# A two-layer hybrid decoder on one core: sums of squares by TensorE, later sums for the second half, rotary swaps from ScalarE's queue, and other distances and rates

## The chip, the core and the metric

The kernel runs on one core of a Trainium2 chip. The core's engines are TensorE (PE, with its weight loads shown as PEld), VectorE (DVE), ScalarE (ACT), GpSimd (POOL) and SyncE (SP), which here only issues DMAs. Each engine runs its own instructions strictly in the order in which they stand in its queue and waits on semaphores for the others. The metric is the device time of one execution in microseconds.

## The reference

A trunk of two layers over 512 tokens of width 1024, followed by a final RMSNorm. Cut to what matters:

```python
for l in range(DEPTH):                       # 2
    sh1, sc1, g1, sh2, sc2, g2 = split(silu(c) @ ada_w[l] + ada_b[l], 6)
    h = rmsnorm(x, norm_mix_g[l]) * (1.0 + sc1) + sh1
    u = h @ w_in[l]                          # 1024 -> 2564
    fq, fk, fv, ff, pu, rq, rk, rv, rg, cu = split(u)
    y_fox  = forgetting attention, 4 heads x 64, log-sigmoid(ff) summed along time as a bias
    y_pool = causal means over 2, 4, 8, 16 tokens, minus the input, times a 64x64 matrix per group
    y_ret  = chunked retention, 4 heads x 64: rope(rq), rope(rk), decay, group norm, silu(rg)
    y_conv = silu(layernorm(causal depthwise conv, 31 taps, of a * sigmoid(gate)))
    x = x + g1 * (concat(y_fox, y_pool, y_ret, y_conv) @ w_out[l])
    h = rmsnorm(x, norm_ffn_g[l]) * (1.0 + sc2) + sh2
    x = x + g2 * ((silu(h @ ffn_w1[l]) * (h @ ffn_w3[l])) @ ffn_w2[l])
return rmsnorm(x, final_g)
```

All inputs and outputs are float32.

## The kernel before

The activations lie transposed: `xT` holds eight chunks of 128 channels (k = 0 to 7) by 512 tokens. Every large product is made of three matmuls in a fast 32-bit format (`mm3`): each operand is split into a rounded half (`yh`, `wh`, `ah`) and a remainder (`yl`, `wl`, `al`), and the products high by high, high by low and low by high are summed in a bank of PSUM. One tile of weights is fetched by SP into `raw` (two buffers), rounded by ScalarE into `wh` (L179) and subtracted by VectorE into `wl` (L184, "weight split"); four such tiles are held. A product of 512 tokens over 8 chunks is 24 matmuls (`one`); `group` does four products over the two halves of the tokens (0 to 255, 256 to 511), so that the second half can still be in the making while the first is used.

**Norms.** Three norms stand between the large products: one ahead of each feed-forward part and one between the layers (the last, final norm is made in another way). `Norm.chunk` is called when a chunk of `xT` is done. For each half of the tokens it squares the chunk on ScalarE and adds it to `acc` on VectorE (L524), eight chunks in a row. The sum over the 128 channels that are left is a matmul with a column of ones (`token_sums`, tile `aux`), then a power on GpSimd (`r`), then `spread` copies it to all partitions by matmuls with the identity. `finish` scales `xT` (L494, tile `qk`), adds the shift and rounds on ScalarE (L503, `yh`) and takes the remainders on VectorE (L507, `yl`). `sums` and `finish` are not run at once: they are put into `pending` with a count, and `flush(n)` takes n off the counts at fixed places between the matmuls. So a count sets where among TensorE's matmuls the sums and the spread stand. `finish` follows the sums by 24.

**Side work in the mixer part.** The four mixers are Python generators that run beside the projections. At each `slot()` a generator advances by its rate (`r_...` for layer 0, `q_...` for layer 1), whole steps at a time; `finish_bg` runs what is left of it on the spot. `conv_gen` issues the 31 taps for two tiles on VectorE (L819, tile `hc`), one tap a step, then mean, variance, scale and swish (L827 to L842). The output projection (`do_o`) starts with `finish_bg([cg])`. `fox_gen` computes the log of the forget gate (`log_forget`, tiles `ff`, last operation L859), makes four empty steps, sums it along time by matmuls (4x128), sends the result through DRAM (`cumd`) back as rows on all partitions (tiles `ah`, `al`), adds the causal mask (L885, `cumD`) and then runs scores (L900, L904), exponentials (L909), normalisation (L911), transposes and products with v. In layer 0 a further generator computes the gates of `ada_w` with TensorE, one column of `aux` a step (from tile `pw`), and adds the bias on VectorE (L357, `mod`) after eight.

**Rotary swaps.** `rope` needs a copy of its tile with the 32-row blocks exchanged in pairs. Four DMAs of 32 x 512 make it (`rx`, L965), issued by the engine that `KN["RD"]` names; then three VectorE operations follow (L966 to L968), and a fourth (L970) for the queries.

**Order.** From the end of layer 0's first projections on, TensorE's matmuls keep the order of the program; the other engines' queues are ordered by a scheduler that simulates the program when it is built.

Of the kernel before, what the change touches and what calls it, by code (L numbers as in the profile page):

```python
# [13 lines left out]
ALU = mybir.AluOpType  # L14
# [32 lines left out]
def trunk(ctx, tc, x, c, positions, ada_w, ada_b, norm_mix_g, norm_ffn_g, w_in, fox_fb,  # L47
# [52 lines left out]
    def f(ap):  # L100
        return ap.bitcast(F32)
# [400 lines left out]
    def mod_hi(l, i, k, u, v, y):  # L502
        A.activation(yh[k][:, u:v], y, AF.Identity, bias=shift(l, i, k), scale=1.0)  # L503

    def mod_lo(l, i, k, u, v, y):
        sh = shift(l, i, k)
        V.scalar_tensor_tensor(out=yl[k][:, u:v], in0=y, scalar=sh, in1=f(yh[k][:, u:v]), op0=ALU.add, op1=ALU.subtract)  # L507

    class Norm:
        def __init__(self, l, i):  # L510
# [2 lines left out]
        def chunk(self, k, a, b):  # L513
            for (u, v) in HALF:
                if u < a or v > b:
                    continue
                n = self.cnt.get(u, 0)
                if n == 0:
                    self.acc[u] = tmp("P", H2)
                    A.activation(self.acc[u], xT[:, k, u:v], AF.Square)  # L520
                else:
                    sq = tmp("PT", H2)
                    A.activation(sq, xT[:, k, u:v], AF.Square)
                    V.tensor_tensor(out=self.acc[u], in0=self.acc[u], in1=sq, op=ALU.add)  # L524
# [903 lines left out]
```

## Time and profile before

| what | value |
|---|---|
| median of 3 runs | 1266.83 us (1265.42 to 1266.85) |
| profiled execution | 1266.76 us, its span 1265.0 us |
| busy: PE, DVE, ACT, POOL | 1208.8, 733.4, 411.6, 75.0 us |
| mean granted clock of TensorE | 0.972 |
| mixer part of layer 0, of layer 1 | about 76 to 235 us, 693 to 830 us |
| norms | about 265 to 304, 640 to 682, 858 to 898 us |

A busy time is the union of the spans of an engine's instructions; where TensorE stands for over a few tenths of a microsecond, the row of the next instruction names the wait in brackets, and the engine and line that ended it. In rows of the timeline the columns are start, length (us), engine, line, operation, output<-inputs, form and count; "x4" merges four instructions, and a matmul of float32 operands is shown as two. In the table of windows each engine's busy time is followed by its count, and the last three figures are the granted clock, the DMA engines' busy share and GB/s. In lists of waits the figures are the total, the number of waits and the longest.

### The profile page before, as it was taken

What the parts mean: (1) busy time and instruction counts of PE and PEld (TensorE: products, weight loads), DVE (VectorE), ACT (ScalarE), POOL (GpSimd) and SP (SyncE); (2) the same over time, 40 slices, a digit from 0 to 9 for tenths busy, and PEclk for the clock granted to TensorE, in tenths of its full rate; (3) what the DMA queues carried; (4) which work ended last, traced back from release to release, by engine and by line L of the source; (5) the groups of instructions that cost most, each with busy time, mean ns of one, the idle gap of its engine ahead of it and who ended that gap; (6) DMA issues with size and microseconds to landing.
All of it is one profiled execution on the core that took longest, in us unless ns stands there. A gap on an engine that the chain in (4) does not pass through costs nothing.

```text
span 1265.0 us, 17346 instructions
## 1 busy us (share of the span) xinstructions
PE 1208.8 (96%) x6781; PEld 1008.6 (80%) x6781; DVE 733.4 (58%) x1295; ACT 411.6 (33%) x690; POOL 75.0 (6%) x146
## 2 busy tenths in 40 slices
PE   9998899897999999999998899997999999999997
PEld 8786677697888888888898777777988888888877
DVE  6777964466987355473465997657653333342333
ACT  5434344243332222122233344524332122222222
POOL 5411011001000000000000000100100000000000
PEclk8999899798999999999998999999999999999999
DMA  9766742124987345353232342122543333233321
GB/s 308 191 179 191 179 135 70 46 72 127 290 291 240 100 136 171 102 177 95 88 82 72 97 122 78 51 83 83 165 136 97 87 100 98 86 99 100 94 73 67
DMA packets 240873, 160.07 MB, mean 127 GB/s; under 512 B 7094, under 2 KB 221328, under 8 KB 240792
## 3 DMA queue, kind: packets, MB, share of 16 engines
q1 hardware_dynamic: 240616, 158.89, 42.6%
q8 instruction: 53, 0.87, 0.3%
q14 instruction: 28, 0.23, 0.1%
q10 hardware_dynamic: 176, 0.08, 0.0%
HBM read 154.74 MB, written 2.11 MB: 124 GB/s over the span
## 4 chain that ended last, share of the span: by engine, by line
PE 83%; DVE 7%; issue 1%; DMA 1%; ACT 1%; SPq 0%; POOL 0%; DVEq 0%; ACTq 0%
PE mm L59 74%; PE sm L59 7%; DVE wl L184 2%; DVE hc L819 1%; PE aux L59 1%; PE sm L64 1%; DVE yl L507 1%; DVE qk L494 1%; DMA al<-cumd 1%; DMA raw<-in_w_in 0%; DVE xT L1141 0%; ACT wh L179 0%; DVE P L524 0%; DVE hc L827 0%; DMA rx<-rx 0%
## 5 line engine op out<-in xcount | busy, mean ns | idle before, releaser
L179 ACT CAST wh<-raw 128x1024 fp32r<-128x1024 f32 (+3 forms) x196 | 198.7, 1014 | 612.1 <-PE mm L59 458.9
L59 PE MATMUL mm<-yh,wh 128*128 128x512 f32 (+1 forms) x984 | 376.0, 389 | 0.0
L59 PE MATMUL mm<-yh,wl 128*128 128x512 f32 (+1 forms) x984 | 371.1, 381 | 0.0
L59 PE MATMUL mm<-yl,wh 128*128 128x512 f32 (+1 forms) x984 | 350.2, 378 | 0.2 <-DVE yl L507 0.2
L184 DVE TENSOR_TENSOR wl<-raw,wh 128x1024 fp32r<-128x1024 f32 (+3 forms) x196 | 231.9, 1183 | 163.9 <-ACT wh L179 153.6
L59 PEld LDWEIGHTS mm<-yh,wh 128*128 128x128 f32 x984 | 189.4, 193 | 39.7 <-issue 6.1
L59 PEld LDWEIGHTS mm<-yh,wl 128*128 128x128 f32 x984 | 190.4, 194 | 36.6
L59 PEld LDWEIGHTS mm<-yl,wh 128*128 128x128 f32 x984 | 176.8, 189 | 34.6 <-issue 1.0
L59 PE MATMUL mm<-ah,wh 128*128 128x512 f32 (+1 forms) x508 | 188.0, 370 | 1.7 <-ACT ah L551 1.7
L59 PE MATMUL mm<-al,wh 128*128 128x512 f32 (+1 forms) x508 | 186.9, 368 | 0.0
L59 PE MATMUL mm<-ah,wl 128*128 128x512 f32 (+1 forms) x508 | 186.5, 367 | 0.0
L1141 DVE SCALAR_TENSOR_TENSOR xT<-mm,mod,xT 128x512 f32<-128x512 f32 (+1 forms) x84 | 56.6, 674 | 142.8 <-PE mm L59 142.8
L59 PEld LDWEIGHTS mm<-ah,wh 128*128 128x128 f32 x508 | 96.5, 190 | 19.2 <-ACT ah L551 2.4
L59 PEld LDWEIGHTS mm<-al,wh 128*128 128x128 f32 x508 | 96.5, 190 | 17.0 <-DVE al L552 0.4
L59 PEld LDWEIGHTS mm<-ah,wl 128*128 128x128 f32 x508 | 96.5, 190 | 16.8
L1331 DVE TENSOR_TENSOR t<-t,mm 128x512 f32<-128x512 f32 x42 | 28.8, 686 | 108.0 <-PE mm L59 107.9
L819 DVE SCALAR_TENSOR_TENSOR hc<-hp,cwT,hc 128x512 f32<-128x512 f32 x120 | 84.6, 745 | 0.1
L364 DVE SCALAR_TENSOR_TENSOR acs<-ada,cact,acs 128x512 f32<-128x512 f32 x98 | 73.4, 749 | 6.5 <-DMA ada<-in_ada_w 4.6
L473 POOL TENSOR_TENSOR r<-r,mhalf 128x2 f32<-128x2 f32 (+3 forms) x16 | 19.1, 1191 | 621.6 <-DVE r L481 603.3
L59 PE MATMUL mm<-wh,yh 128*128 128x256 f32 (+1 forms) x128 | 37.9, 296 | 0.0
L59 PE MATMUL mm<-wl,yh 128*128 128x256 f32 (+1 forms) x128 | 36.7, 287 | 0.0
L59 PE MATMUL mm<-wh,yl 128*128 128x256 f32 (+1 forms) x128 | 36.7, 287 | 0.0
(251 smaller groups left out, 1161.8 us busy)
## 6 DMA issues: line engine op xcount, KB each, us to landing
raw<-in_ffn_w SPq DMA_DIRECT2D x104, 512.0 KB, 3.9
ada<-in_ada_w SPq DMA_DIRECT2D x80, 512.0 KB, 5.4
raw<-in_w_in SPq DMA_DIRECT2D x32, 512.0 KB, 4.3
raw<-in_ffn_w SPq DMA_DIRECT2D x32, 448.0 KB, 3.5
ad<-in_ada_w SPq DMA_DIRECT2D x32, 256.0 KB, 5.5
raw<-in_w_out SPq DMA_DIRECT2D x32, 256.0 KB, 3.0
raw<-in_w_in SPq DMA_DIRECT2D x4, 520.0 KB, 4.6
xn<-in_x SPq DMA_DIRECT2D x4, 512.0 KB, 5.6
```

The source lines that it names most:

```text
L59: m = nc.tensor.matmul(*a, **kw)
L64: m = nc.tensor.transpose(*a, **kw)
L179: A.copy(h[:, 0:n], raw)
L184: V.tensor_tensor(out=lo[:, 0:n], in0=raw, in1=f(h[:, 0:n]), op=ALU.subtract)
L364: V.scalar_tensor_tensor(out=acc, in0=r, scalar=ck, in1=acc, op0=ALU.mult, op1=ALU.add)
L473: G.tensor_tensor(out=out_, in0=ms, in1=mhalf[:, 0:ms.shape[-1]], op=ALU.pow)
L494: V.scalar_tensor_tensor(out=y, in0=xT[:, k, u:v], scalar=gs[l][i][:, k:k + 1], in1=rs, op0=ALU.mult, op1=ALU.mult)
L507: V.scalar_tensor_tensor(out=yl[k][:, u:v], in0=y, scalar=sh, in1=f(yh[k][:, u:v]), op0=ALU.add, op1=ALU.subtract)
L819: V.scalar_tensor_tensor(out=hcs[j], in0=hps[j][:, t:t + S], scalar=cwT[:, l, j, t:t + 1], in1=hcs[j], op0=ALU.mult, op1=ALU.add)
L1141: V.scalar_tensor_tensor(out=xT[:, n, u:v], in0=b[:, u:v], scalar=mod[l][:, gcol + n:gcol + n + 1], in1=xT[:, n, u:v], op0=ALU.mult, op1=A ...
L1331: V.tensor_tensor(out=t_, in0=t_, in1=b3, op=ALU.mult)
```

## The change

`chunk` squares the last two chunks (k = 6 and 7 in order of arrival) into tiles of their own (`rP`) and adds them nowhere; `sums` then runs three matmuls for each 128 tokens, one for `acc` and one for each of the two tiles, instead of one. The count ahead of the sums is 56 for the second half of the tokens instead of 18. `rope`'s four DMAs are issued by ScalarE. `r_conv` is 1.6 instead of 1.3, and `fox_gen` makes 5 empty steps in layer 0 and 6 in layer 1 instead of 4. `mod_lo` has an engine argument that no call sets.

```diff
-KN = {... 'RD': 'sync', ... 'r_conv': 1.3, ...}
+KN = {... 'RD': 'scalar', ... 'r_conv': 1.6, ...}
...
-    def mod_lo(l, i, k, u, v, y):
+    def mod_lo(l, i, k, u, v, y, eng="V"):
...
                 if n == 0:
-                    self.acc[u] = tmp("P", H2)
-                    A.activation(self.acc[u], xT[:, k, u:v], AF.Square)
-                else:
+                    self.acc[u] = [tmp("P", H2)]
+                    A.activation(self.acc[u][0], xT[:, k, u:v], AF.Square)
+                elif n < KD - 2:
                     sq = tmp("PT", H2)
                     A.activation(sq, xT[:, k, u:v], AF.Square)
-                    V.tensor_tensor(out=self.acc[u], in0=self.acc[u], in1=sq, op=ALU.add)
+                    V.tensor_tensor(out=self.acc[u][0], in0=self.acc[u][0], in1=sq, op=ALU.add)
+                else:
+                    sq = tmp("rP", H2)
+                    A.activation(sq, xT[:, k, u:v], AF.Square)
+                    self.acc[u].append(sq)
                 self.cnt[u] = n + 1
                 if n + 1 == KD:
-                    pending.append([18, lambda u=u, v=v: self.sums(u, v)])
+                    pending.append([18 if u == 0 else 56, lambda u=u, v=v: self.sums(u, v)])
 
         def sums(self, u, v):
-            r = token_rsqrt(token_sums(self.acc[u], 2), 2, 1.0 / D, KN["TR"])
+            pt = aux_cols(2)
+            for t in range(2):
+                for q, src in enumerate(self.acc[u]):
+                    PE.matmul(pt[:, t:t + 1], src[:, t * P:(t + 1) * P], ones[:, 0:1], start=q == 0,
+                              stop=q == len(self.acc[u]) - 1)
+            r = token_rsqrt(pt, 2, 1.0 / D, KN["TR"])
             pending.append([24, lambda: self.finish(u, v, r)])
...
         lf = log_forget(l, v[:, :, 256:260])
-        for _ in range(4):
+        for _ in range(5 + l):
             yield
```

**TensorE, the norm ahead of layer 0's feed-forward part.** `yh_94` to `yh_101` are the eight chunks of `yh`; `mm_2902` to `sm_2905` are the four products of the group; `aux` takes the sums. Before, the second half's sums stand after chunk 3 of the first two products:

```order
L59 MATMUL mm_2903<-yh_97,wh_2787 128x256
L59 MATMUL mm_2903<-yh_97,wl_2789 128x256
L59 MATMUL aux<-ones,P_2634 128x1 x2
L59 MATMUL mm_2902<-yh_98,wh_2638 128x256
L59 MATMUL mm_2902<-yh_98,wl_2640 128x256
```

After, they stand behind chunk 4 of the other two:

```order
L59 MATMUL sm_2905<-yh_98,wh_2895 128x256
L59 MATMUL sm_2905<-yh_98,wl_2897 128x256
L59 MATMUL aux<-ones,P_2634 128x1
L59 MATMUL aux<-ones,rP_2879 128x1
L59 MATMUL aux<-ones,rP_2900 128x1
L59 MATMUL aux<-ones,P_2634 128x1
L59 MATMUL aux<-ones,rP_2879 128x1
L59 MATMUL aux<-ones,rP_2900 128x1
L59 MATMUL mm_2904<-yh_99,wh_2858 128x256
```

The sums moved from behind 16 matmuls of the group to behind 52, and there are six instead of two; the same holds in the other two norms.

**TensorE, the end of layer 0's mixer part.** `mm_2349` is the last projection, `hc` the conv tiles, `t_2416` its squares, `mm_2465` the first output product. Before:

```order
L59 MATMUL mm_2349<-yh_101,wl_1819 128x512
L59 MATMUL aux<-sel,pw_2383 128x1
L59 MATMUL sm_2411<-hc_1030,ones 128x512
L59 MATMUL sm_2411<-hc_1031,ones 128x512
L59 MATMUL sm_2422<-ident,r_429_2273 64x128 x8
L59 MATMUL aux<-ones,t_2416 128x1 x4
L59 MATMUL sm_2444<-ident,r_462_2441 128x128 x4
L59 MATMUL mm_2465<-ah_2345,wh_1986 128x512
```

After, the conv mixer's spread (`r_431_2278`) stands here, ahead of the last projection (`mm_2375`):

```order
L59 MATMUL aux<-sel,pw_2269 128x1
L59 MATMUL sm_2320<-ada_2194,cact 32x128 x8
L59 MATMUL sm_2331<-ident,r_431_2278 128x128 x4
L59 MATMUL sm_2354<-ident,r_376_2026 64x128 x8
L59 MATMUL sm_2368<-pl_2220,pw_2215 128x512
L59 MATMUL mm_2375<-yh_94,wh_1813 128x512
```

The mean, the sums and the spread moved out from between the last projection and the first output product: 60, 36 and 24 projection matmuls now lie between them and that product.

**VectorE, the first normalised scores of layer 0.** `hc` rows are conv taps, `rx` and `qk` rows rotary passes, ISA rows scores with their row minima; the last two rows of each piece are the normalisations of the first two heads. Before:

```order
L184 TENSOR_TENSOR wl_1213<-raw_1209,wh_1211 128x1024
L819 SCALAR_TENSOR_TENSOR hc_1030<-hp_792,cwT,hc_1030 128x512
L966 TENSOR_TENSOR qk_1217<-rx_1215,cos_t 128x512
L819 SCALAR_TENSOR_TENSOR hc_1031<-hp_797,cwT,hc_1031 128x512
L910 RECIPROCAL mx_1231<-mx_1231 128x1
L910 RECIPROCAL mx_1237<-mx_1237 128x1
L819 SCALAR_TENSOR_TENSOR hc_1030<-hp_792,cwT,hc_1030 128x512
L967 TENSOR_TENSOR rx_1218<-rx_1218,sin_t 128x512
L819 SCALAR_TENSOR_TENSOR hc_1031<-hp_797,cwT,hc_1031 128x512
L911 TENSOR_SCALAR P_1230<-P_1230,mx_1231 128x128
L911 TENSOR_SCALAR P_1236<-P_1236,mx_1237 128x128
```

After (its lines are ten further on: L910 and L914 are scores, L921 the normalisation):

```order
L829 SCALAR_TENSOR_TENSOR hc_1030<-hp_792,cwT,hc_1030 128x512
L829 SCALAR_TENSOR_TENSOR hc_1031<-hp_797,cwT,hc_1031 128x512
L910 ISA P_1344,mx_1345<-sm_1340,cumD_1226 128x128
L910 ISA mx_1345 128x1
L914 ISA P_1344,mx_1345<-sm_1340,ah_201_1168 128x128
L914 ISA mx_1345 128x1
L910 ISA P_1352,mx_1353<-sm_1341,cumD_1228 128x128
L910 ISA mx_1353 128x1
L914 ISA P_1352,mx_1353<-sm_1341,al_202_1169 128x128
L914 ISA mx_1353 128x1
L921 TENSOR_SCALAR P_1249<-P_1249,mx_1250 128x128
L921 TENSOR_SCALAR P_1255<-P_1255,mx_1256 128x128
```

The second pair's four score passes moved ahead of the first pair's normalisations; the ada bias add L357, which stood twelve rows behind them, now stands seven rows above this piece. In ScalarE's queue the swaps now stand as four DMAs each, right behind the copy that they read for the first, and behind exponentials and copies of the ada steps for the next three.

More of the change, by code (lines that the diff above doesn't have):

```diff
@@ L34 @@
 TW = 528
-KN = {'GA': 3, 'GA1': 3, 'TR': 'V', 'NH': 6, 'NH1': 6, 'ST': ((0, 1), (1, 1), (2, 2), (4, 1), (5, 1), (6, 1), (7, 1)), 'MO': 'rk rq rv pu rg o o o o', 'MO1': 'rk rq rv pu rg o o o o', 'GK': 4, 'RD': 'sync', 'MM': 3, 'SM': 4, 'FB': 1, 'FB1': 1, 'OUTP': 0.0, 'FRONT': 1, 'FRONT1': 0, 'r_rot': 2, 'r_ada': 0.9, 'r_conv': 1.3, 'r_fox': 1, 'r_ret': 1, 'r_pool': 1, 'r_adaV': 0.4, 'q_conv': 1.3, 'q_fox': 1, 'q_ret': 1, 'q_pool': 1, 'q_adaV': 1, 'bP': 4, 'bPT': 2, 'bt': 3, 'brx': 2, 'bmx': 6, 'br8': 4, 'bpl': 3, 'brP': 4, 'bada': 3, 'bacs': 2, 'NR': 2, 'NW': 4, 'N1': 2, 'N11': 1, 'YLG': 9, 'SC': ('AVPPPGPA', 'GGPAVVPP', 'VVVVVVPP', 'VVVVVGVP', 'AAVPAVVP', 'VVVVVVVP', 'VVVVVVVP', 'AAVPAVVP'), 'SH': ('AVAPPPPP', 'VPPPPPAP', 'AAGAAAPP', 'AAAAAAPP', 'AAAAAAGP', 'AVVGAAVG', 'AAAAAAPP', 'AAAAAAPP'), 'MS': '', 'OF': {'lc': -1.907, 'lwq': -2.817, 'lw': -2.364, 'lh': -2.036, 'sc': -1.65, 'ds': 0.034, 'sh': -2.846, 'pc': -0.763, 'mc': -2.466, 'ph': -0.991, 'mh': 0.907, 't': 0.871, 'yh': -1.858, 'yl': 0.927, 'wh': -0.208, 'wl': -2.386, 'whq': -1.469, 'wlq': -0.219, 'mm': 0.333, 'mq': -0.566, 'dq': 0.84}, 'KB': (-4.084, -0.552, 1.672, 3.163, 4.202, 4.915, 6.134, 7.492), 'OA': (1, 0, 2, 3), 'OA1': (0, 1, 3, 2), 'OB': (1, 2, 0, 3), 'OB1': (1, 3, 0, 2), 'OUTP1': 3.0}
@@ new lines @@
+KN = {'GA': 3, 'GA1': 3, 'TR': 'V', 'NH': 6, 'NH1': 6, 'ST': ((0, 1), (1, 1), (2, 2), (4, 1), (5, 1), (6, 1), (7, 1)), 'MO': 'rk rq rv pu rg o o o o', 'MO1': 'rk rq rv pu rg o o o o', 'GK': 4, 'RD': 'scalar', 'MM': 3, 'SM': 4, 'FB': 1, 'FB1': 1, 'OUTP': 0.0, 'FRONT': 1, 'FRONT1': 0, 'r_rot': 2, 'r_ada': 0.9, 'r_conv': 1.6, 'r_fox': 1, 'r_ret': 1, 'r_pool': 1, 'r_adaV': 0.4, 'q_conv': 1.3, 'q_fox': 1, 'q_ret': 1, 'q_pool': 1, 'q_adaV': 1, 'bP': 4, 'bPT': 2, 'bt': 3, 'brx': 2, 'bmx': 6, 'br8': 4, 'bpl': 3, 'brP': 4, 'bada': 3, 'bacs': 2, 'NR': 2, 'NW': 4, 'N1': 2, 'N11': 1, 'YLG': 9, 'SC': ('AVPPPGPA', 'GGPAVVPP', 'VVVVVVPP', 'VVVVVGVP', 'AAVPAVVP', 'VVVVVVVP', 'VVVVVVVP', 'AAVPAVVP'), 'SH': ('AVAPPPPP', 'VPPPPPAP', 'AAGAAAPP', 'AAAAAAPP', 'AAAAAAGP', 'AVVGAAVG', 'AAAAAAPP', 'AAAAAAPP'), 'MS': '', 'OF': {'lc': -1.907, 'lwq': -2.817, 'lw': -2.364, 'lh': -2.036, 'sc': -1.65, 'ds': 0.034, 'sh': -2.846, 'pc': -0.763, 'mc': -2.466, 'ph': -0.991, 'mh': 0.907, 't': 0.871, 'yh': -1.858, 'yl': 0.927, 'wh': -0.208, 'wl': -2.386, 'whq': -1.469, 'wlq': -0.219, 'mm': 0.333, 'mq': -0.566, 'dq': 0.84}, 'KB': (-4.084, -0.552, 1.672, 3.163, 4.202, 4.915, 6.134, 7.492), 'OA': (1, 0, 2, 3), 'OA1': (0, 1, 3, 2), 'OB': (1, 2, 0, 3), 'OB1': (1, 3, 0, 2), 'OUTP1': 3.0}
@@ L503, in mod_hi @@
         A.activation(yh[k][:, u:v], y, AF.Identity, bias=shift(l, i, k), scale=1.0)
-    def mod_lo(l, i, k, u, v, y):
+    def mod_lo(l, i, k, u, v, y, eng="V"):
         sh = shift(l, i, k)
-        V.scalar_tensor_tensor(out=yl[k][:, u:v], in0=y, scalar=sh, in1=f(yh[k][:, u:v]), op0=ALU.add, op1=ALU.subtract)
+        (G if eng == "G" else V).scalar_tensor_tensor(out=yl[k][:, u:v], in0=y, scalar=sh, in1=f(yh[k][:, u:v]),
+                                                      op0=ALU.add, op1=ALU.subtract)
     class Norm:
```

## The prediction

> **What bounds the kernel now.** I read the shares and the clock line of the page, then the waits of TensorE over the whole span, then a table by stage, then the rows inside four stages.
>
> ```profile
> PE 1208.8 (96%) x6781; PEld 1008.6 (80%) x6781; DVE 733.4 (58%) x1295; ACT 411.6 (33%) x690; POOL 75.0 (6%) x146
> PEclk8999899798999999999998999999999999999999
> PE 83%; DVE 7%; issue 1%; DMA 1%; ACT 1%; SPq 0%; POOL 0%; DVEq 0%; ACTq 0%
> ```
>
> TensorE is the bound: 96% busy, 83% of the chain that ended last. Time can come only from its waits and from its clock, which dips below full in some slices. This lists what it waits for:
>
> ```profile
> PE aux L59 <- DVE P L524: 18.3, 3, 6.5
> PE sm L59 <- DVE ff L859: 6.2, 2, 4.1
> PE aux L59 <- DVE t L832: 3.1, 1, 3.1
> PE aux L59 <- DMA rx<-rx: 2.9, 1, 2.9
> PE mm L59 <- ACT ah L551: 1.7, 1, 1.7
> ```
>
> Three waits for the norm's adds (L524), two for the forget gate's logarithm (L859), the tail of the conv mixer (L832, L551), one named after a rotary swap: 32.2 us, and all of them stand where the diff works. The stages around them:
>
> ```profile
> core 0: us, PE busy (x) PEld busy (x) DVE busy (x) ACT busy (x) POOL busy (x), PEclk, DMA share, GB/s
> 127.00:140.00 13.00, 10.39 (x63) 7.38 (x64) 11.78 (x33) 3.33 (x9) 0.37 (x2) 0.74 0.61 150
> 140.00:155.00 15.00, 14.55 (x141) 11.51 (x140) 15.00 (x41) 6.51 (x17) 0.84 (x3) 1.00 0.74 193
> 200.00:219.60 19.60, 18.68 (x161) 14.56 (x160) 6.81 (x13) 6.09 (x13) 1.90 (x3) 1.00 0.23 70
> 219.60:235.40 15.80, 9.74 (x46) 7.03 (x45) 8.80 (x16) 6.66 (x11) 1.21 (x2) 0.66 0.12 36
> 235.40:265.00 29.60, 29.60 (x114) 23.52 (x115) 12.63 (x15) 4.73 (x6) 0.00 (x0) 0.89 0.23 71
> 720.00:735.00 15.00, 14.90 (x69) 11.40 (x70) 15.00 (x24) 2.15 (x4) 0.00 (x0) 0.90 0.32 102
> ```
>
> The third figure from the end is the granted clock: 0.74 behind the 2.9 us wait, which ends at 129.6, 0.66 and 0.89 around the conv tail, 0.90 after the layer-1 logarithm. So a wait costs its length and then some matmuls at a lower clock. VectorE is full in 140 to 155 and in 720 to 735, and a third busy just ahead of the conv tail.
>
> **The norms: squares and the later sums.** Rows of the first norm (after layer 0's output projection):
>
> ```profile
> 275.27 0.55 PE L59 MATMUL aux<-ones,P 128*128 128x1 f32 x4
> 275.68 0.37 PE L59 MATMUL mm<-ah,wh 128*128 128x256 f32 x1
> 284.59 0.28 PE L59 MATMUL mm<-yh,wh 128*128 128x256 f32 x1
> 284.71 0.28 PE L59 MATMUL mm<-yh,wl 128*128 128x256 f32 x1
> 291.46 1.01 PE L59 MATMUL aux<-ones,P 128*128 128x1 f32 x4 [6.48 <-DVE P L524]
> 292.70 0.41 PE L59 MATMUL mm<-yh,wl 128*128 128x256 f32 x1
> 292.91 0.41 PE L59 MATMUL mm<-yh,wh 128*128 128x256 f32 x1
> 304.15 0.28 PE L59 MATMUL mm<-yh,wh 128*128 128x256 f32 x1
> 288.01 1.22 DVE L184 TENSOR_TENSOR wl<-raw,wh 128x1024 fp32r<-128x1024 f32 x1
> 289.93 1.48 DVE L524 TENSOR_TENSOR P<-P,PT 128x256 f32<-128x256 f32 x3
> 297.77 3.22 DVE L494 SCALAR_TENSOR_TENSOR qk<-xT,gs,sm 128x256 f32<-128x256 f32 x8 [5.09 <-PE sm L59]
> 300.91 3.25 DVE L507 SCALAR_TENSOR_TENSOR yl<-qk,mod,yh 128x256 fp32r<-128x256 f32 x8
> ```
>
> TensorE does 16 matmuls of the first half, then stands 6.5 us at the second half's sums, whose last three adds sit on VectorE behind a weight split (288.01) and the first half's remainders. Matmuls start 0.12 us apart before (284.59 to 284.71) and 0.21 after (292.70 to 292.91). The matmuls of the second half start at 304.15, and its first 24 end at 304.15 + 24 x 0.118 = 307.0.
>
> Moved: the sums stand behind 52 matmuls instead of 16, the spread behind 24 more as before. Two of the three adds at 289.93 go (0.4 us each). Added: six sum matmuls for two; two took 0.41 us (275.27 to 275.68), so four more are 0.8 us a half. I follow the new order with these durations. The 16 matmuls that end at 284.8 began at 284.83 - 16 x 0.118 = 282.9; now 0.8 us late, at 283.7. Its matmuls of the fourth tile begin 35 places on, at 287.9, but that tile's split ends about 289.4: 1.5 us of new wait, which the old stall hid. Then 16 matmuls to the sums, at 291.4. The one add left follows the split and two remainders, 289.4 + 0.9 + 0.4 = 290.7, so no wait. Sums 1.2, 24 matmuls 2.8, spread 0.4: 295.8; 20 matmuls: 298.2. Scaling (8 x 0.40) runs from 296.0, the rounded halves follow at that pace, the last at 299.8, just when wanted. The remainders run 299.2 to 302.5 and are wanted from 300.1 to 300.9: another 1.6 us. The first 24 matmuls end near 302.6 against 307.0: 4.4 us. The other two norms have the same code and waits that make 18.3 with this one; taken as 4.3 each, three norms give 13 us. Ends: 7.4 each if neither new wait appears (6.5, plus 22 matmuls x 0.095, plus 0.4 on the slow sums, less 1.6), 2 each if both double: 6 to 22.
>
> The clock: after 6.5 us of standing, 22 matmuls ran at half rate. The Trainium skill ("TensorE: Matmul & The Clock Gate", Part 1) says an idle window of about 3.4 us halves the clock, and about 3.4 us of work restores it; the 0.21 us agree, but the 2.9 us wait was followed by 0.74 as well. By that rule alone a 2.9 us wait would cost no clock, the 13 x 0.26 below would not come back, and the sum would be some 3 us smaller; the row decides, and I keep it.
>
> **Conv tail, layer 0 (r_conv 1.3 to 1.6).**
>
> ```profile
> 219.80 1.96 PE L59 MATMUL sm<-hc,ones 128*128 128x512 f32 x4
> 221.70 1.09 PE L59 MATMUL sm<-ident,r 128*64 128x128 f32 x16
> 229.05 2.07 PE L59 MATMUL sm<-ident,r 128*128 128x128 f32 x8 [1.34 <-POOL r L473]
> 230.78 0.77 PE L59 MATMUL mm<-ah,wh 128*128 128x512 f32 x1
> 241.79 0.43 PE L59 MATMUL mm<-ah,wl 128*128 128x512 f32 x1
> 235.33 1.30 DVE L552 TENSOR_TENSOR al<-hc,ah 128x512 fp32r<-128x512 f32 x2
> ```
>
> Today the generator has steps left when the projection wants its result, so mean, variance, scale and swish are forced out in a row with TensorE waiting. Between 219.80 and 241.79 it does the mean (1.9), a spread for retention (1.1), four sums (4 x 0.2 = 0.8), the conv spread (1.7 at half clock, so 0.9), and 20 matmuls of 512 columns (twice 0.118: 4.7): 9.4 us of work in 22.0. Now mean, sums and spread stand 60, 36 and 24 projection matmuls ahead. The 24 take 5.6 us, with some 2 us of small ones among them; spread to the last remainder takes 229.05 to 236.6, 7.6 us, and VectorE there was a third busy (6.81 of 19.60). So nearly all 12.6 us come back; I take 11.5, leaving 1 us for VectorE finishing pool, retention and conv together. Ends: 8 and 12.6.
>
> **Forget gate (5 + l steps).**
>
> ```profile
> 103.48 0.38 PE L59 MATMUL sm<-cs,ff 128*4 128x128 f32 x2 [2.13 <-DVE ff L859]
> 720.10 0.59 PE L59 MATMUL sm<-cs,ff 128*4 128x128 f32 x2 [4.10 <-DVE ff L859]
> 730.57 0.69 DVE L885 TENSOR_TENSOR cumD<-al,cs 128x512 f32<-128x512 f32 x1
> 739.40 0.29 DVE L900 CUSTOM_DVE_ANT_0 P<-sm,cumD 128x128 f32<-128x128 f32 x1
> PEld aux L59 <- DVE mod L357: 3.1, 1, 3.1
> L965 SPq DMA_DIRECT2D rx<-rx x32: 507/584/1576, 114.7 to 766.0; - x32
> SPq L965 <- DVE qk L968: 7.5, 3, 3.3
> ```
>
> Layer 1: 24 more matmuls (5.6 us) stand ahead of the cumulative sum, over the 4.1 us. Its scores keep their place, so the path from the sum through DRAM to the scores loses 5.6 us of cover; its last decay add ended at 731.3 and the scores read it at 739.4, so that holds. Gain 4.1 + 15 x 0.10 of clock = 5.6; VectorE is full behind it but its queue holds fewer taps ahead of the scores, so 5. Ends 1 and 5.6.
>
> Layer 0: one step more (12 projection matmuls and an ada step, 3.7 us) covers the 2.1. Here the scores move with it. Between decay and the first normalised scores VectorE's queue now holds four more score passes (0.3 each, as at 739.40), two rotary passes and a tap (0.65 each, as in the pair at 235.33): 3.2 us, so I put a wait of 2 us at the transposes. In return the 2.9 us wait goes: the page names the swap as its end, but the weight load of the same matmul names the ada bias add L357, which stood behind scores and a weight split and now stands ahead of them. Before: 2.1 + 2.9 + 13 x 0.26 of clock = 8.4; after: 2 + 2 of clock. Gain 4, ends -4 (the wait at the transposes as long as the norm's) and 8.4.
>
> **Swaps on ScalarE.** 32 issues of 0.58 us, four to a swap: 18.7 us move from SP to ScalarE, with SP's waits for L968 (7.5 us) in front of three of them. SP is relieved: weight and ada loads no longer queue there, worth nothing on the path since no wait of TensorE names a weight load here. On ScalarE, weight casts, score exponentials and PSUM copies queue behind each swap's 2.3 us. ScalarE is busy 6.51 of 15.00 in the densest stage. I take 2 us lost; ends 0 and 19. The Trainium skill ("DMA: Bandwidth & Descriptors", Issuing engines are not separate DMA queues) says another issuing engine saves only issue time; by that alone the swaps gain nothing, which is what the sum has.
>
> The other edits change no instruction (the engine argument is unused).
>
> **Sum.** 13 + 11.5 + 5 + 4 - 2 = 31.5 us off the profiled execution's 1266.76 (span 1265.0), which is 0.07 us under the median of 1266.83: 1235 us.
>
> **Rivals.** (1) VectorE becomes the bound in the mixers: full in 140 to 155 and 720 to 735, it keeps TensorE where it was, and the 9 us of the gate terms go: 1244. Against: its queue is no longer ahead of the weight splits in layer 1. (2) The second half of the norm comes too late: spread at 295.8 leaves 2.4 us before its matmuls; if scaling starts 4.4 us late (splits or casts in between), each norm gives nothing: 1248. (3) Slower: ScalarE is held by the swaps. If each stops it for 2.3 us and three also for L968, and all of it reaches TensorE, 18.7 + 7.5 = 26 us are lost where I took 2: 1259, and eight clock drops of 2.1 us (22 x 0.095, as after the norm's wait) make it 1276. It decides once a swap delays a PSUM copy by more than the 3 to 4 us that stand between a copy and its reader. (4) The waits have other releasers than named (the adds merely came last) and move on unchanged: 1266.
>
> **Chances.** Forecast 1235 (1225 to 1242) 0.65; rival 1 0.17; rival 2 0.10; rival 3 0.04; rival 4 0.04. The range holds forecast and rival 1 and rival 2: 1225 to 1250. Within 0.2% (2.5 us) is about what a measurement here can't tell from no change. Faster 0.93, same 0.03, slower 0.04.
>
> **What would show it.** After: the three L524 waits gone, with 1 to 2 us waits of TensorE for a split (L184) and the remainders (L507) in their place; no wait for L832 and a clock near 1.0 where 0.66 stood; no wait for L859; a wait of about 2 us at a transpose in layer 0 near 127; swaps on ScalarE's queue. A wait of TensorE for ScalarE copies of over 1 us at each swap, or a clock under 0.9 inside the norms, would make it wrong.

## The result, and the profile after

The changed kernel takes 1255.95 us (median of 4 runs, 1253.05 to 1256.45) against 1266.12 us for the kernel before (4 runs): a ratio of 0.9918 [0.9897, 0.9939]. By the ratio it is 10.4 us faster, where 31.5 were forecast. Two executions far slower than all others (one of the version q_nc below at 3004 us, which is also the one that its trace shows, so that trace is not used, and one of the kernel before at 4869 us) are left out of the ratios. The profiled execution took 1255.64 us, its span is 1253.9 us, its mean granted clock 0.981 (0.972 before).

The shares and the clock line of the page of after, and the longest waits of TensorE over its span (total, number, longest):

```profile
PE 1211.4 (97%) x6829; PEld 1009.3 (80%) x6829; DVE 726.6 (58%) x1283; ACT 410.7 (33%) x690; POOL 75.2 (6%) x146
PEclk7999898999999999999999999999999999999999
```

```profile
PE sm L59 <- DVE wl L184: 6.3, 3, 2.3
PE sm L64 <- DVE P L921: 5.3, 4, 2.9
PE aux L59 <- ACT pw L430: 4.5, 2, 2.4
PE sm L59 <- DVE qk L980: 2.9, 1, 2.9
PE sm L59 <- DVE mx L914: 1.4, 1, 1.4
```

All five waits that the prediction listed (32.2 us) are gone. In their place stand these five kinds, 20.4 us, of which the first was forecast. (Line numbers behind L526 are ten higher than before: L911 is now L921, L859 is L869.) TensorE is still the bound.

Cut at the same instructions in both traces, the stages changed by these lengths (from the rows' start times):

| stage | change, us |
|---|---|
| mixer part of layer 0, with output projection | -5.4 |
| first norm | -3.1 |
| second norm (between the layers) | -1.2 |
| mixer part of layer 1, with output projection | +1.0 |
| third norm | -1.9 |
| both feed-forward parts | 0.0 |

So the first layer's mixer part and the three norms improved, and layer 1's mixer part got worse. Of the 5.4 us of layer 0, some 1.5 are not the change's: before runs at half clock from 74.5 to 78 us, ahead of all that was edited, and after does not there, while p_conv and n56 below do. First the **norm ahead of layer 0's feed-forward part**, rows of the timeline of after:

```profile
283.09 1.22 DVE L184 TENSOR_TENSOR wl<-raw,wh 128x1024 fp32r<-128x1024 f32 x1
284.36 0.39 PE L59 MATMUL sm<-yh,wl 128*128 128x256 f32 x1 [2.02 <-DVE wl L184]
286.48 0.28 PE L59 MATMUL aux<-ones,P 128*128 128x1 f32 x2
287.74 0.36 PE L59 MATMUL mm<-yh,wh 128*128 128x256 f32 x1
293.48 0.28 PE L59 MATMUL mm<-yh,wh 128*128 128x256 f32 x1
295.54 2.61 PE L59 MATMUL mm<-yl,wh 128*128 128x256 f32 x8
297.98 0.28 PE L59 MATMUL mm<-yh,wh 128*128 128x256 f32 x1
```

The sums no longer wait, and take 1.26 us (286.48 to 287.74). The fourth tile's split comes 2.02 us late, and eight matmuls with remainders take 2.44 us (295.54 to 297.98) for some 0.94 of work: the two new waits that the prediction named. It had put them at 1.5 and 1.6 us; they are 2.0 and 1.5.

**The mixer part of layer 0**, a table by stage and the rows of TensorE's new waits:

```profile
127.00:142.00 15.00, 11.73 (x82) 8.32 (x81) 12.73 (x40) 4.99 (x13) 0.90 (x2) 0.95 0.77 202
142.00:156.00 14.00, 13.91 (x118) 11.82 (x119) 13.20 (x32) 4.42 (x13) 1.05 (x2) 0.81 0.48 133
200.00:215.00 15.00, 13.61 (x105) 11.15 (x106) 6.18 (x24) 4.02 (x10) 3.86 (x7) 0.79 0.24 73
230.00:275.00 45.00, 45.00 (x275) 39.52 (x274) 25.89 (x43) 12.13 (x22) 0.90 (x2) 1.00 0.23 72
```

```profile
117.79 0.38 PE L59 MATMUL aux<-sel,pw 128*128 128x1 f32 x2 [2.35 <-ACT pw L430]
124.46 0.38 PE L59 MATMUL aux<-sel,pw 128*128 128x1 f32 x2 [2.11 <-ACT pw L430]
140.89 0.87 PE L64 MATMUL sm<-ident,P 128*128 128x128 f32 x3 [2.88 <-DVE P L921]
182.41 0.64 PE L59 MATMUL sm<-ada,cact 128*32 128x128 f32 x16 [1.39 <-DVE mx L914]
201.02 0.64 PE L59 MATMUL sm<-ada,cact 128*32 128x128 f32 x16 [1.53 <-issue]
```

The conv tail is clean (230 to 275: TensorE busy throughout at clock 1.00, where 0.66 and 0.89 stood). The first half of the mixer is not: two waits for a copy on ScalarE (L430), one of 2.88 us for the normalised scores (L921), and two further on. The prediction had put a wait of 2 us at a transpose near 127, for passes that stand ahead of the normalisation. The one at 140.89 is another: VectorE itself stands for the second swap shortly ahead of it.

```profile
133.37 0.69 DVE L977 TENSOR_TENSOR rx<-rx,sin_t 128x512 f32<-128x512 f32 x1 [2.27 <-DMA rx<-rx]
```

The copies came late for this reason (ScalarE's rows; ACTq is its queue issuing DMAs):

```profile
109.78 7.65 ACTq L975 DMA_DIRECT2D rx<-rx  x4
116.92 0.51 ACTq L975 DMA_DIRECT2D rx<-rx  x1
117.47 0.27 ACT L430 COPY pw<-sm 128x128 f32<-128x128 f32 x1 [7.73 <-DMA ah<-cumd]
```

The first swap's four DMAs last from 109.78 to 117.43; at the 0.58 us of an issue on SP before, they would take 2.3. The fourth starts at 116.92, when the broadcast of the forget gate's sums from DRAM (`ah<-cumd`, issued by SP) has landed, and the copy behind it is put down to that transfer too. ScalarE's queue stands still for the 5.3 us of difference.

**Layer 1**: the wait for the logarithm (4.10) is gone; two others appeared, for the scores and for a rotary:

```profile
741.41 0.77 PE L64 MATMUL sm<-ident,P 128*128 128x128 f32 x4 [1.48 <-DVE P L921]
757.77 0.49 PE L59 MATMUL sm<-qk,qk 64*128 64x128 f32 x4 [2.88 <-DVE qk L980]
```

### The profile page after: what moved, and what is told of

Same layout as the page of the kernel before. It is cut to its first block, busy times and chain, and to the rows that moved or that the text cites. A ratio compares the mean times of both kernels' runs of the same rounds, so it can differ in the third digit from the quotient of the medians.

```text
span 1253.9 us, 17394 instructions
## 1 busy us (share of the span) xinstructions
PE 1211.4 (97%) x6829; PEld 1009.3 (80%) x6829; DVE 726.6 (58%) x1283; ACT 410.7 (33%) x690; POOL 75.2 (6%) x146
## 3 DMA queue, kind: packets, MB, share of 16 engines
HBM read 154.74 MB, written 2.11 MB: 125 GB/s over the span
## 5 line engine op out<-in xcount | busy, mean ns | idle before, releaser
L59 PE MATMUL mm<-yh,wl 128*128 128x512 f32 (+1 forms) x984 | 366.9, 378 | 0.0
L59 PE MATMUL mm<-yl,wh 128*128 128x512 f32 (+1 forms) x984 | 355.5, 380 | 0.2
L59 PEld LDWEIGHTS mm<-yh,wl 128*128 128x128 f32 x984 | 187.5, 191 | 36.7
```

The costliest lines, as they stand in the source:

```text
L59: m = nc.tensor.matmul(*a, **kw)
```

## The experiments

Diffs are against the kernel before unless another is named. A ratio is to runs of the kernel before on the same chip, with its 95% interval; one ratio can be told from another to some 0.003, or 4 us. In microseconds a ratio is taken times 1265.

**Each part alone.** p_norm has the diff's `chunk` and `sums`, with

```diff
-                    pending.append([18, lambda u=u, v=v: self.sums(u, v)])
+                    pending.append([18 if u == 0 else 56, lambda u=u, v=v: self.sums(u, v)])
```

> The kernel before with the norms' part alone (squares of the last two chunks by TensorE, the second half's sums at 56). In the trace of the whole change the three norms give 3.1, 1.2 and 1.9 us from the first half's sums to the second half's second product, 6.2 us together where I had predicted 13. Theory N1 (the split of the fourth tile comes late in VectorE's queue whatever else is changed): a wait of TensorE of 2.0 to 2.3 us for L184 in each norm, and 5 to 8 us off the kernel before: 1258 to 1261. Theory N2 (the splits are late only because the rest of the change shifts VectorE's queue): the L184 waits are under 1 us, the gain is 11 to 14 us, about 1253.

Measured: 1261.34 us, 0.9969 [0.9954, 0.9985]: 3.9 us, a little less than theory N1 gave. The waits are N1's; the split is late whatever stands around the norms:

```profile
PE sm L59 <- DVE wl L184: 6.3, 3, 2.3
```

is p_norm's row of waits, as in after.

```diff
-KN = {... 'r_conv': 1.3, ...}
+KN = {... 'r_conv': 1.6, ...}
```

> The kernel before with r_conv 1.6 alone. Theory C1 (the tail comes back as predicted): 8 to 12.6 us gained, 1254 to 1258, no wait at the sums of the conv squares, no low clock between 220 and 245. Theory C2 (the taps issued sooner take VectorE's time from the scores and weight splits before it): the tail's 9 us are gained and 3 to 8 us of it lost between 110 and 200, so 1258 to 1264.

Measured: 1255.62 us, 0.9928 [0.9907, 0.9948]: 9.1 us (theory C1), nearly as much as the whole change's 10.4.

```diff
-        for _ in range(4):
+        for _ in range(5 + l):
```

> The kernel before with the longer distance ahead of the cumulative sum alone (5 empty steps in layer 0, 6 in layer 1). My prediction: 9 us gained, 1257. Theory S (the swaps on ScalarE take away what the gates give): here, with the swaps on SP, 6 to 9 us are gained, and no wait of over 1.5 us stands at the transposes of the scores. Theory V (the scores come closer to other VectorE work and wait there): both waits for the logarithm go, but waits of 1.5 to 3 us for the normalised scores (L911) come in both layers; the gain is 0 to 3 us, 1263 to 1267.

Measured: 1271.52 us, 1.0059 [1.0038, 1.0080]: slower by 7.5 us, which neither theory gave. The steps cost where they should have gained. In this trace most of it stands in layer 1: from the first sums of the norm ahead of it to those of the norm behind it 221.9 us pass, 216.3 in before. TensorE's waits there grew by 1.1 us only; low clock took 9.6 us of its busy time instead of 4.8 (the last section says how this is counted).

```diff
-KN = {... 'RD': 'sync', ...}
+KN = {... 'RD': 'scalar', ...}
```

> The kernel before with the swaps issued by ScalarE alone. In the trace of the whole change the fourth DMA of the first swap starts 5.3 us late, when the broadcast of the cumulative sums has landed, and the copy of the ada sums behind it is waited for by TensorE for 2.4 us. Theory S: 5 to 10 us lost, 1271 to 1276, with waits of TensorE for L430. Theory V (the swaps cost ScalarE time that nobody waits for): within 2.5 us of the kernel before.

Measured: 1276.49 us, 1.0090 [1.0073, 1.0107]: slower by 11.4 us, theory S's time. Its sign did not come: no wait of TensorE for L430 stands among those of over 0.4 us, and no swap of layer 0 holds ScalarE longer than 3.01 us (the first 2.52). The new waits are for scores on VectorE (1.76 us at 140.81, 2.05 at 143.27) and for copies of transposed scores.

**In pairs.** q_nc is norms and conv, q_fs the steps and the swaps.

> The norms' part and r_conv 1.6 together, swaps on SP and 4 empty steps as before. Alone they measured 3.9 us (0.31%) and 9.1 us (0.72%) off. Theory I1 (these two are independent, and the other two parts, which cost 7.5 and 11.4 us alone, cancel each other inside the whole change): they add, 13 us off, 1251 to 1254. Theory I2 (norms and conv gain only together with the rest): 5 us off or less, 1260.

Measured: 1249.32 us (median of all four executions), 0.9874 [0.9850, 0.9898]: 15.9 us faster, some 3 more than the two parts alone add up to (theory I1, within the error), and better than the whole change by 5.6.

> The longer distance and the swaps on ScalarE together, norms and conv as before. Alone they cost 7.5 us (0.59%) and 11.4 us (0.90%). Theory I1: together they cost 0 to 5 us, 1265 to 1270. Theory I2: they add, 19 us, 1284.

Measured: 1274.16 us, 1.0064 [1.0041, 1.0088]: 8.1 us slower, between the two theories. The two pairs add up to -7.8, the whole is -10.4: additive within the error. So the change is two halves of opposite sign.

**Which of the two costs more.** a_sync is after with `'RD': 'sync'`; a_fox4 is after with `range(4)`; f0 and f1 are q_nc with one step more in layer 0 and two in layer 1:

```diff
-        for _ in range(4):
+        for _ in range(5 - l):        # f0
+        for _ in range(4 + 2 * l):    # f1
```

> The whole change with the swaps back on SP. Theory S (ScalarE held by the swaps ate what was missing, the fourth DMA waiting 5.3 us for the broadcast's landing): 8 to 12 us faster than the whole change, 1244 to 1248. Theory I1 (without the swaps' shift the longer distance costs its 7.5 us): 3 to 6 us slower than the whole change, 1259 to 1262.

Measured: 1254.84 us, 0.9926 [0.9900, 0.9951]: neither theory's time.

> The whole change with 4 empty steps in both layers, swaps on ScalarE. Theory S: the waits for the logarithm come back (2.1 and 4.1 us), 6 to 9 us slower than the whole change, 1262 to 1265. Theory I1: the swaps alone cost their 11.4 us against norms and conv alone: 1262 to 1265 too, with waits of 1 to 2 us for normalised scores at 125 and 140. Theory V (the distance costs by bringing the scores closer to other VectorE work, and the swaps cost little): 2 to 6 us faster than the whole change.

Measured: 1257.37 us, 0.9948 [0.9929, 0.9966]: 4 us slower than the whole change, which again no theory gave.

> Norms and conv together (1249) with 5 empty steps in layer 0 and 4 in layer 1. My prediction had layer 0's step gain 4 us: 1245. Theory V (the scores come closer to other work on VectorE and ScalarE): the waits of 2.1 and 2.9 us go, waits of 2.3 us for L430 and 1 to 1.5 us for scores come in their place, 1249 to 1252.

Measured: 1255.41 us, 0.9930 [0.9907, 0.9954]: slower still than theory V had it.

> Norms and conv together (1249) with 4 empty steps in layer 0 and 6 in layer 1. My prediction had layer 1's steps gain 5 us: 1244. Theory V: the wait of 4.1 us for the logarithm goes, waits of 1.9 us for the normalised scores near 743 and of 2.9 us for a rotary pass near 766 come, each followed by low clock: 1251 to 1255.

Measured: 1252.73 us, 0.9903 [0.9873, 0.9934]: theory V.

On top of q_nc (0.9874) the swaps alone cost 9 us, the step in layer 0 7, the steps in layer 1 4 (no more than the error), all steps 7, and everything 6. The costs don't add: with the steps in, putting the swaps back on SP changes nothing (0.9926 against 0.9918). The trace of f0 shows why, in rows of TensorE, ScalarE and SP:

```profile
127.76 0.59 PE L59 MATMUL aux<-sel,pw 128*128 128x1 f32 x2 [3.19 <-ACT pw L430]
125.16 0.59 ACT L1221 COPY rx<-mm 128x512 f32<-128x512 f32 x1 [4.97 <-DMA rx<-rx]
125.77 1.28 ACT L919 ACT_TABLE_LOAD   x1
127.46 0.25 ACT L430 COPY pw<-sm 128x128 f32<-128x128 f32 x1
115.20 0.57 SPq L889 DMA_DIRECT2D ah<-cumd  x1
117.30 2.51 SPq L975 DMA_DIRECT2D rx<-rx  x4
```

With the sum a step later its broadcast stands on SP's queue (115.20) just ahead of a swap (117.30). ScalarE's copy of the next tile into `rx` waits 4.97 us for a swap, the table load and an exponential follow, and the copy that TensorE wants (L430) stands behind them. So swap and broadcast meet on SP as they do through ScalarE's queue in after, and end in the same 2 to 3 us wait. (That the swap lands late because of the broadcast ahead of it is read from the order of the rows, and was not tested alone.) The wait is the smaller part of the loss: layer 0's mixer part is 7.9 us longer in f0's trace than in f1's, which leaves it alone, 2.5 of them TensorE's waits and 4.8 low clock. The rows of f1 in layer 1, where the logarithm's wait had been taken away:

```profile
725.87 0.33 PE L64 MATMUL sm<-ident,P 128*128 128x128 f32 x1 [2.34 <-DVE P L921]
750.34 1.64 PE L59 MATMUL sm<-qk,qk 64*128 64x128 f32 x16 [2.49 <-DVE qk L980]
```

That is 4.8 us of new waits for 4.1 (the logarithm's wait of 2.1 in layer 0 stays), and layer 1's part is as long as f0's, where its steps are not changed: 215.9 us in both.

**The sum later, the scores kept in place** (on n56, below): the step that stood behind the broadcast's DMAs is taken out in layer 0.

```diff
-        for _ in range(4):
+        for _ in range(5 - l):
...
-        yield
+        if l:
+            yield
```

> The version with conv and the later sums alone (1246.2), layer 0's cumulative sum one step later, but one empty step fewer behind it, so that the scores keep their place. Theory P (the scores' place costs: the last of them run out of projections to hide behind): the wait of 2.1 us for the logarithm goes and no waits come between 150 and 215: 1242 to 1246. Theory Q (the sum's way through DRAM loses its cover): the scores wait for the broadcast, 3 us or more at the first transposes: 1248 to 1252.

Measured: 1249.16 us, 0.9879 [0.9855, 0.9903], against n56's 0.9857: no gain, theory Q's time. No wait over 1 us stands between 150 and 215 us now, where f0 has three (1.13 at 157.63, then 1.39 and 1.54), but two stand ahead:

```profile
119.83 1.08 PE L59 MATMUL sm<-ada,cact 128*32 128x128 f32 x16 [4.40 <-issue]
129.15 0.59 PE L64 MATMUL sm<-ident,P 128*128 128x128 f32 x2 [4.19 <-DVE P L912]
```

Theory Q's cause is not shown, though. VectorE waits 5.88 us for the broadcast, as in before (5.93), and ScalarE's copy waits 5.86 us for the swap that now follows the broadcast directly, with the exponentials behind it. Which of the two holds the scores stays open; a step taken out behind the broadcast has at any rate not paid for the one put in ahead of it.

**Why the swaps cost on ScalarE.** When the issuing engine changes, the scheduler also orders VectorE and ScalarE in another way. pin_d and pin_da are q_nc with the swaps on ScalarE and a written-out order that holds VectorE (pin_d), or VectorE and ScalarE (pin_da), to that of q_nc:

```diff
-KN = {... 'RD': 'sync', ...}
+KN = {... 'RD': 'scalar', ...}
...
+        for order in PIN.values():
+            for p, q in zip(order, order[1:]):
+                tc.add_manual_dep(ins[q], p, NOSYNC, reason="pin")
```

> Norms and conv with the swaps on ScalarE (1257.4), but all instructions of VectorE and ScalarE beside the swaps themselves in the order that they have with the swaps on SP (1249.3). Only the 32 issues are moved. Theory S (the held queue costs): 1254 to 1259, with waits of TensorE for ScalarE's copies (L430, L932). Theory V (the changed order costs): 1248 to 1251, without the waits of 1.7 to 2.1 us at 128 and at 142 to 146.

Measured: 1254.75 us, 0.9929 [0.9907, 0.9951]: theory S's time.

> The same with VectorE's order alone forced back, ScalarE's left to the build. Theory S: 1254 to 1259. Theory V, if VectorE's order is the whole of it: 1248 to 1251; if ScalarE's counts too: between, 1251 to 1255.

Measured: 1254.31 us, 0.9924 [0.9909, 0.9940]: theory S's time too, or the one between.

Of the 9 us that the swaps cost on q_nc (0.9948), some 6 to 7 remain with the order held and 2 to 3 come back; the second figure is within the error. Rows of pin_da (lines two higher than in after; the traced execution took 1260.61 us, above the median):

```profile
114.55 4.00 ACTq L977 DMA_DIRECT2D rx<-rx  x4
709.73 0.59 PE L61 MATMUL sm<-cs,ff 128*4 128x128 f32 x2 [5.16 <-DVE ff L871]
750.81 0.93 PE L61 MATMUL sm<-PT,v 128*64 128x128 f32 x8 [2.11 <-ACT PT L934]
```

The first swap holds ScalarE 4.0 us, and in layer 1 the logarithm's wait is 5.16 instead of 4.10 and a copy of transposed scores (PT) is 2.11 late. From the totals one would say that the held queue carries most of the loss. But what remains is not the same loss. The table has one trace each: layer 0's mixer part from TensorE's wait at 73 us to the first norm's first sums, and the stretch with layer 1's, from the second norm's first sums to the third's; in brackets what low clock took of it. Swaps on SP are read from f1 for layer 0 and from f0 for layer 1, each of which leaves that part as in q_nc.

| us | layer 0 | layer 1 |
|---|---|---|
| swaps on SP | 189.2 (6.6) | 215.9 (2.0) |
| on ScalarE, order of the scheduler (a_fox4) | 196.8 (8.0) | 216.1 (1.7) |
| on ScalarE, VectorE's order held (pin_d) | 190.2 (6.6) | 219.0 (4.3) |
| on ScalarE, both orders held (pin_da) | 193.0 (8.3) | 221.2 (3.1) |

With the scheduler's own order the loss, 7.6 us, stands in layer 0, and layer 1 shows next to none. With VectorE's order held 6.6 of the 7.6 are gone, and so are the waits of 1.7 to 2.1 us at 130 and at 143 to 146 that theory V named, though the swaps still stand on ScalarE. No swap of layer 0 is held there (2.53 us for the first, where after has 7.65). So layer 0's loss goes with VectorE's changed order. Forced into the other order, layer 1 loses 3 to 5 us that it did not lose before; the rows of pin_da show a late ScalarE there, but how much of this is the held queue, the held order or the clock stays open.

n_pool issues them from GpSimd instead (on n56, below): `'RD': 'gpsimd'`.

> The version with conv and the later sums alone (1246.2), swaps issued by GpSimd, which is busy for 6% only. Theory S (ScalarE held by the issues): no loss, 1245 to 1248. Theory V (another issuer alters VectorE's order at the scores, whichever it is): 4 us lost or more, 1250 to 1256, with the waits for normalised scores near 127 and 142 that ScalarE's swaps brought.

Measured: 1253.83 us, 0.9920 [0.9893, 0.9946], 8 us more than n56: theory V's time, but not its waits for scores. The longest wait is

```profile
156.06 2.08 PE L59 MATMUL sm<-qk,qk 64*128 64x128 f32 x16 [6.00 <-DVE qk L970]
```

which is for a rotary pass on VectorE. The loss stands in layer 0 again (197.5 us, 190.4 in n56). TensorE's waits for work of GpSimd are 1.1, 0.4 and 0.3 us in all, so a loss of 8 us does not need an issuing engine whose held queue keeps TensorE waiting.

**The norms taken apart.** n56 has r_conv 1.6 and the count of 56, with all adds on VectorE as before; n18 has r_conv 1.6 and the squares on TensorE, with the count left at 18.

> r_conv 1.6 and the second half's sums at 56, but all seven adds of squares on VectorE and two sum matmuls a half, as before; compare norms and conv together, 1249. Theory N3 (the later place does the work, the squares by TensorE only cost six small matmuls for two): in the trace of the norms' part a half's sums last 1.25 us for 0.41, 0.84 x 6 = 5.0 us; the adds end after the last remainders, just when the sums come: 3 to 5 us faster, 1244 to 1246, a wait for L524 of at most 0.6 us in each norm. Theory N4 (the adds held TensorE, as the wait's name said): waits of 1 to 3 us for L524 stay in each norm, 1250 to 1258.

Measured: 1246.17 us, 0.9857 [0.9826, 0.9889]: theory N3's time, and no wait for L524 of over 0.3 us.

> Norms and conv together, but the sums of both halves at 18 as before: the squares by TensorE alone. Theory N3: the stalls stay at 5 to 6 us each (the last add still follows the split and the remainders), and the small matmuls cost 5 us: 1255 to 1259, close to or slower than conv alone (1255.6). Theory N4: the stalls shrink to under 3 us each, 1247 to 1250.

Measured: 1255.31 us, 0.9929 [0.9905, 0.9952], as conv alone (0.9928) and as theory N3 had it. The old stall is still there, as long in the third norm; in the second, TensorE waits 1.89 us for a square on ScalarE instead. The third's:

```profile
277.64 0.59 PE L59 MATMUL aux<-ones,P 128*128 128x1 f32 x2 [5.40 <-DVE P L525]
```

So the later place alone is worth 9 us on p_conv, and the squares on TensorE nothing: with the sums at 18 the shorter chain of adds shortens the first norm's wait from 6.5 to 5.4 us and the four added sum matmuls take that back (0.85 us a half); with the sums at 56 there is no wait left to shorten, and the six halves cost 6 x 0.85 = 5.1 us by their rows (1.26 for 0.41). n56 against q_nc, 0.9857 to 0.9874, is 2 us, within the error.

**The two waits that are left.** g_split (on n56) runs the third product's 16 matmuls ahead of the fourth's, so that the fourth tile's split is wanted 14 matmuls (1.65 us) later; g_both runs in addition, for the second half of the tokens, the rounded products of two tiles before their remainders:

```diff
+                    pairs = [(k, i) for k in range(nk) for i in (i0, i0 + 1)]
+                    if i0:
+                        pairs = [(k, i) for i in (i0, i0 + 1) for k in range(nk)]
...
-                    for k in range(nk):
-                        PE.matmul(banks[i][:, a:b], h[:, k], ...)
-                        PE.matmul(banks[i][:, a:b], lo[:, k], ...)
+                    for q in (i, i + 1) if i % 2 == 0 else ():
+                        hq, lq = ws[q]
+                        for k in range(nk):
+                            PE.matmul(banks[q][:, a:b], hq[:, k], ...)
+                            PE.matmul(banks[q][:, a:b], lq[:, k], ...)
```

> The version with conv and the later sums alone (1246.2), and in each norm's first half the third product's 16 matmuls ahead of the fourth's instead of in turns, so that the fourth tile's split is wanted 14 matmuls (1.65 us) later. Theory N5 (that split is what the later sums ran into): the waits for L184 fall from 2.0 to 2.3 us to under 0.6 us, and with them the low clock behind them: 3 to 6 us faster, 1240 to 1243. Theory N6 (something else on VectorE is wanted next, the adds or the remainders): the wait moves on to L524 or L507, less than 2 us gained.

Measured: 1247.60 us, 0.9837 [0.9780, 0.9895]. The split's wait falls from 6.3 to 1.3 us over the three norms, and 3.4 us of wait for the adds (L527 here) come back, as theory N6 had it; against n56 the 2.5 us by the ratio are within the error:

```profile
PE aux L59 <- DVE P L527: 3.4, 3, 1.6
PE sm L59 <- DVE wl L184: 1.3, 3, 0.6
```

> As the run before, and in the second half the rounded products of two tiles ahead of their remainder products, so that the remainders are wanted 16 matmuls (1.9 us) later. In the trace of the whole change eight remainder matmuls took 2.44 us for 0.91 in each norm. Theory N5: another 1.5 us a norm, 4.5 us: 1235 to 1239. Theory N6: no further gain, 1240 to 1246.

Measured: 1238.29 us (1232.98 to 1244.85), 0.9797 [0.9751, 0.9843]: the best version, ahead of both kernels, and some 8 us ahead of n56 with intervals that just meet. Its traced execution took 1232.98 us, and 7.5 of the 13.5 us that this is shorter than n56's are low clock. The remainder matmuls of both tiles now run at their own pace, 16 in 2.05 us, where after took 2.44 for 8:

```profile
286.85 2.05 PE L59 MATMUL mm<-yl,wh 128*128 128x256 f32 x16
```

## Why the prediction was wrong

The sign was right, the size was not: 10.4 us for 31.5. 8.6 us of the difference lie in norms and conv (24.5 forecast, 15.9 measured together), 12.6 in steps and swaps (7 gained forecast, 5.6 lost).

**Norms (13 forecast).** The mechanism was right in each step that it named: L524 gone, a wait for the split, 0.85 us a half for the sums, a wait for the remainders. The stages gained 3.1, 1.2 and 1.9, 6.2 in all, just inside the ends of 6 to 22 that the prediction gave; alone 3.9. The mis-sized step is "1.5 us of new wait, which the old stall hid": it is 2.02, 2.25 and 2.02 us. In the first norm the scaling besides begins 1.1 us later than worked out. The step "taken as 4.3 each" overlooked that the second norm's old stall was 5.37 us and not 6.5, and that the new wait can cost clock again: the prediction counted the clock that came back (22 matmuls at half rate) and none that is newly lost, which the second and the third norm have. The second norm's rows show it, with matmuls 0.22 us apart behind the wait (0.12 in the first norm):

```profile
659.75 0.58 PE L59 MATMUL sm<-yh,wl 128*128 128x256 f32 x1 [2.25 <-DVE wl L184]
660.13 0.42 PE L59 MATMUL mm<-yh,wh 128*128 128x256 f32 x1
660.35 0.41 PE L59 MATMUL mm<-yh,wl 128*128 128x256 f32 x1
```

**Conv tail (11.5 forecast, ends 8 and 12.6).** Right: 9.1 us alone, and L832 and L551 are gone. What misses is within the error; low clock ahead of the tail, 0.79 in 200 to 215 us in after and 0.77 in p_conv, among small matmuls that had stood elsewhere, is part of it.

**Forget gate, layer 1 (5).** "The scores read it at 739.4, so that holds" did hold: in after 2.4 us are left between the last decay add and the first score.

```profile
721.31 0.69 DVE L895 TENSOR_TENSOR cumD<-al,cs 128x512 f32<-128x512 f32 x1
724.38 0.28 DVE L910 CUSTOM_DVE_ANT_0 P<-sm,cumD 128x128 f32<-128x128 f32 x1
```

The step that failed is the next, "its queue holds fewer taps ahead of the scores, so 5", which took 0.6 us off for a full VectorE. The 4.1 us went, but VectorE, which from 720 to 759 never stands longer than 0.45 us in after, gave them back at the scores and at a rotary (2.34 and 2.49 in f1, 1.48 and 2.88 in after). This is rival 1, in layer 1.

**Forget gate, layer 0 (4, ends -4 and 8.4).** The waits of 2.1 and 2.9 us went. The forecast wait at a transpose near 127 did not come: f0 and p_fox, which have the step with the swaps on SP, have no wait for normalised scores of over 1 us in layer 0, and the 2.88 of after comes from a swap, so that it lies close to 2 is luck. The failed step is that the sum's way was followed through VectorE alone. Missing are SP's and ScalarE's queues, where the broadcast meets the swap (f0: 3.19 us), and "2 of clock": low clock takes 4.8 us more in f0 than in f1, where the prediction had 3.4 come back and 2 lost. And the scores that move back run out of projections to hide behind: 1.39 and 1.53 us at 182.41 and 201.02.

**Swaps (-2, ends 0 and 19).** Alone they lose 11.4 us, on q_nc 9. The step that failed is "I take 2 us lost": it prices the issues on ScalarE's queue, and has no term for the other order that the scheduler gives VectorE when the issuer changes. With VectorE held to the old order, 6.6 of layer 0's 7.6 us come back. It also bounded a swap by its 2.3 us of issue, where in after the first one held ScalarE for 7.65. Rival 3 had the sign right, at less than half its price; that its mechanism, the held queue, is what costs is not shown, since p_swap loses 11.4 us with no swap of layer 0 over 3.01. (Its 7.5 us of waits for L968 are layer 0's alone; over the whole execution they are 15.2 in six waits.) That relieving SP is worth nothing fits all runs. The Trainium skill ("DMA: Bandwidth & Descriptors", Issuing engines are not separate DMA queues) says that another engine saves only issue time; the runs agree that nothing is gained, and show a loss that it does not speak of.

Rival 2 (scaling too late, nothing gained by the norms) did not happen: the spread's matmuls wait for nothing in after. Rival 4 is what g_split shows on a small scale: behind the split's wait stood the adds'.

## What to carry to other kernels

Where TensorE waits for a chain on another engine, first move the reader behind independent matmuls; shortening the chain is worth nothing once the reader is late enough (n56 against q_nc), and next check what the matmuls pulled forward now wait for. An empty step that hides a wait at one end takes the cover from the other end of the same chain, so follow the chain through every queue to its last reader, DMA issues included. A DMA on a compute engine's queue can cost that engine the DMA's wait as well as its issue (7.65 us for four issues in after). And where a scheduler orders the queues, an edit that only names another issuer changes the order of the other engines too: look at what moved there before pricing the issues. One execution's low clock can be as large as the waits in question, so count it apart from them.

## What the hardware showed that was not expected

**The clock drops in fixed windows.** In both traces every stretch of low clock (but the last, which the end cuts) is at half and 1, 2, 3 or 5 times 3.41 us long, and all edges of one execution lie on one grid of 3.413 us. Stretches of after, TensorE's busy time first and the granted clock third from the end:

```profile
280.51:283.92 3.41, 1.83 (x16) 1.63 (x14) 3.41 (x8) 0.99 (x3) 0.00 (x0) 1.00 0.52 154
283.92:287.33 3.41, 2.97 (x26) 2.97 (x26) 1.51 (x4) 0.00 (x0) 0.00 (x0) 1.00 0.51 147
871.01:874.42 3.41, 1.39 (x12) 1.19 (x11) 3.41 (x8) 0.42 (x1) 0.00 (x0) 1.00 0.88 268
874.42:877.84 3.42, 3.42 (x17) 3.42 (x18) 0.92 (x3) 0.00 (x0) 0.00 (x0) 0.50 0.63 192
208.83:212.24 3.41, 3.08 (x34) 2.72 (x35) 0.33 (x2) 0.67 (x3) 1.13 (x2) 1.00 0.00 0
212.24:215.65 3.41, 3.41 (x9) 2.67 (x8) 0.00 (x0) 0.00 (x0) 1.52 (x1) 0.50 0.00 0
```

The first norm's wait of 2.02 us falls across an edge, leaves its window 1.58 us idle, and costs no clock. The third's wait is as long, but leaves its window 2.02 us idle, and the next window runs at half: of its 3.42 us of work half is lost, 1.7 us. The second's 2.25 us leave 1.88 idle and end the same way. Among small matmuls (the fifth row) a window 0.33 us idle was followed by half clock too, so idle time alone does not decide; what does is not shown. The Trainium skill ("TensorE: Matmul & The Clock Gate", Part 1) gives a free-running window of about 3.4 us, and length and grid agree; that an idle window is needed does not agree, since TensorE was busy for 1.39 us or more in each of these.

With the trace cut into stretches of 1 us, before shows 20 windows at half clock and after 13. Weighted with TensorE's busy time (busy time times one less the granted clock, summed over the stretches) the low clock cost 28.3 us in before and 21.6 in after. So the spans' 11.1 us are made up like this: TensorE's idle time (span less busy) falls from 56.2 to 42.5 us, 13.7 less; its busy time rises by 2.6, of which the clock is -6.7, the added sums +5.1, and some 4 stay unassigned (matmuls' ends are modelled). A part of the gain is thus the clock's, and of two waits of 2.02 us one cost 2 us and the other 3.7, by where the grid happened to lie.
